# Reordering the state-space mixer of a decoder trunk into a four-part pipeline with a pinned order

## The chip, the cores and the metric

One core of one Trainium2 chip runs the whole program in one launch. The metric is the device time of a run in microseconds; a kernel's time is the median of its runs.

## The reference

A two-layer trunk over 576 tokens (512 of a prompt and 8 samples of 8 tokens), model width 1024. Order: half-step SwiGLU FFN, mixer, half-step FFN in each layer, a norm ahead of each. The mixer of layer 0 is the state-space mixer (SSD), the one that the change touches:

```python
z, xbc, dt_raw = split(h @ w_in)
xbc = silu(causal_dwconv(xbc))
xs, Bm, Cm = split(xbc)
dt = softplus(dt_raw + dt_bias); A = -exp(a_log)
y_diag = (C B^T * exp(a_i - a_j), tril) @ (x * dt)
y_off  = exp(a_i) * C @ h_start
h_next = h * exp(a_end) + B^T (x * dt * decay_end)
y = (y_diag + y_off + d_skip * x) * silu(z)
y = group_rmsnorm(y) @ w_out
```

There are 32 heads of width 64 in 8 groups (`bt` is B, `ctl` is C of a group), state size 128, chunks of 128 tokens.

## The kernel before, in words

Activations lie transposed, 128 features on the partitions by 576 tokens, and every projection tile is one `acc` accumulation in PSUM: 8 blocks of 128 features, each weight and activation split in a high and a low half and multiplied in three passes, for two halves of 288 tokens, so 48 matmuls of 128x288 (`passes`, L339). There are two `acc` tiles. Small results use `misc`, four PSUM tiles of one bank.

The SSD works by pairs of heads, 16 pairs, two per group g (j = 0, 1). Per pair there is a projection of x with a causal convolution (`conv_in`: ext L636 to L639, tails L641 and L642, bias L645, three taps L647) and one of z (`zproj`, L969). Per group there are one of B and one of C, as columns 16+g and 24+g, with `group()` (L917 to L940: transposes of B, L925, C times B, L936) and the output projection of earlier groups (`outproj`), four tiles in each pair of groups 2, 4 and 6. A group's norm takes the sum of squares `sqacc` (L949, summed by matmuls with ones, L184), an inverse root on VectorE (L189 to L197, the result is `rr`) and transposes that spread it over the partitions (`rbcast`, L218).

`pair()` (L779) is one function. It transposes the old state `nat` (L789) and copies it to `h0t` (L790), multiplies it by C (L795), loads the decay exponents `m`, masks them on GpSimd (L808 to L810), takes their exponential on ScalarE (L813) and multiplies by `cbs` (L814, L815); it transposes x (L824, L777), scales it (L827 to L835), forms the chunk states (L851) and chains them to `ht` (L857), then multiplies `ht` by C (L864), `m` by x (L871, L873), adds up `yt` (L875 to L883, with the z projection inside) and updates `nat` for the samples (L840, L843). Before the first pair, a softplus chain on VectorE (L708 to L723, then L732 to L745, from the projection of dt) gives the tile `rhs`, which `spread()` (L746, first matmul L749) multiplies out and transposes for all pairs.

A scheduler orders the instructions of each engine, each engine then runs its list in order. Only instructions marked by `keep_in_program_order` (`pin`) stay in program order among themselves; in the SSD of the kernel before these are two of the three L864 and all of L871 and L873. The small matmuls of a pair therefore lie in many short runs between the projections.

Of the kernel before, what the change touches and what calls it, by code (L numbers as in the profile page):

```python
# [49 lines left out]
def trunk(ctx, tc, x_prompt, x_sample, state_ssm, state_conv, state_pool,  # L50
# [127 lines left out]
    def rnat(accs, width):  # L178
        pt = misc()
        for c, (t0, n) in enumerate(BLOCKS):  # L180
            for h in range(0, P, 64):
                for i, acc in enumerate(accs):
                    t = t0 + h % n
                    PE.matmul(out=pt[h:h + 64, c:c + 1], lhsT=acc[:, t:t + 64], rhs=ones[:, 0:1], start=i == 0, stop=i == len(accs) - 1)  # L184
        return rstd(pt[:, 0:5], width)
# [28 lines left out]
    def rbcast(r):  # L214
        pt, pt2 = misc(), misc()
        for c, (t0, n) in enumerate(BLOCKS):
            o = pt[:, t0:t0 + n] if c < 4 else pt2[:, 0:n]
            PE.transpose(out=o, in_=r[0:n, c:c + 1].broadcast_to([n, P]), identity=ident[0:n, 0:n])  # L218
        return pt, pt2[:, 0:T - SEQ]
# [114 lines left out]
    def passes(pd, w, acts, first, last):  # L334
        for h in range(2):
            n = 0
            for (wh, wl), (ah, al) in zip(w, acts):
                for lt, a in ((wh, ah), (wh, al), (wl, ah)):
                    PE.matmul(out=pd[:, h, 0:HALF], lhsT=lt, rhs=a[:, h * HALF:(h + 1) * HALF],  # L339
                              start=first and n == 0, stop=last and n == 3 * len(acts) - 1)  # L340
                    n += 1

    def mm(pt, w, acts):
        kn = len(acts)
        for k in range(0, kn, 4):
            passes(pt, w[k:k + 4], acts[k:k + 4], k == 0, k + 4 >= kn)
# [240 lines left out]
    def ssd(tail):  # L587
# [5 lines left out]
        with ExitStack() as st:  # L593
# [31 lines left out]

            def proj(c0, w=None):
                pt = acc_tile()
                mm(pt, w or unit(win[:, :, c0:c0 + P], G), hs)
                return pt

            def conv_in(ct):
# [4 lines left out]
                V.tensor_copy(out=es[:, :, 0:3], in_=cst[:, ct].rearrange("p (b e) -> p b e", e=3))  # L636
# [5 lines left out]
                V.tensor_copy(out=tails[:, ct, 3:27].rearrange("p (b e) -> p b e", e=3), in_=es[:, :, XST - 3:XST])  # L642
                a = wk.tile([P, XW], F32, name="cacc")
                n = XS0 + NB * XST - 3
                S.activation(out=a[:, 0:n], in_=ext[:, 0:n], func=AF.Identity, scale=cw[:, ct:ct + 1], bias=col("cb", ct))  # L645
                for k in range(1, 4):
                    V.scalar_tensor_tensor(out=a[:, 0:n], in0=ext[:, k:k + n], scalar=cw[:, k * 32 + ct:k * 32 + ct + 1], in1=a[:, 0:n],  # L647
                                           op0=ALU.mult, op1=ALU.add)
                return a
# [95 lines left out]
            V.tensor_scalar(out=mh[0:32], in0=mh[0:32], scalar1=hv[0:32, 2:3], scalar2=None, op0=ALU.mult)  # L745
            def spread():  # L746
# [24 lines left out]
            pin = tc.keep_in_program_order  # L771

            def stack(pt, src):
                s3 = wk.tile([P, 2, 3, 32], F32, name="s3", bufs=1)
                S.copy(out=s3, in_=src[:, SEQ:T].rearrange("p (q s) -> p q s", q=2).unsqueeze(2).broadcast_to([P, 2, 3, 32]))
                for q in range(2):
                    PE.transpose(out=pt[0:96, q * P:(q + 1) * P], in_=s3[:, q].rearrange("p a s -> p (a s)"), identity=ident)  # L777

            def pair(g, j, bt, ctl, bnat, bblk, cbs, xst, yt):  # L779
                h0 = 4 * g + 2 * j  # L780
                pr = 2 * g + j
                nat = wk.tile([P, NB, P], F32, name="nat")
                sv = state_ssm[0, :, h0:h0 + 2].rearrange("b h p n -> (h p) b n")
                nc.sync.dma_start(out=nat, in_=sv)
                h0t = wk.tile([P, NB, P], F32, name="h0t", bufs=1)
                for q in range(2):
                    pt = misc()
                    for i in range(4):
                        PE.transpose(out=pt[:, i * P:(i + 1) * P], in_=nat[:, 4 * q + i], identity=ident)  # L789
                    (V.tensor_copy if q else S.copy)(out=h0t[:, 4 * q:4 * q + 4], in_=pt.rearrange("p (b n) -> p b n", n=P))  # L790
                pq = misc()
                for b in range(NB):
                    r = b % 4 * 32
                    o = SEQ + b // 4 * 32
                    PE.matmul(out=pq[r:r + 32, (2 + b // 4) * P:(3 + b // 4) * P], lhsT=ctl[:, o:o + 32], rhs=h0t[:, b], start=True, stop=True)  # L795
                ch = wk.tile([P, 2, P], F32, name="ch", bufs=1)
                V.tensor_copy(out=ch, in_=pq[:, 2 * P:4 * P].rearrange("p (q n) -> p q n", q=2))

                m = wk.tile([P, 2, T], F32, name="m")
                nc.sync.dma_start(out=m, in_=ad[h0:h0 + 2].unsqueeze(0).broadcast_to([P, 2, T]))  # L800
                eb = wk.tile([P, T - P], F32, name="eb", bufs=1)
                for h2 in range(2):
                    nc.sync.dma_start(out=eb[64 * h2:64 * h2 + 64], in_=ed[h0 + h2:h0 + h2 + 1, P:T].broadcast_to([64, T - P]))

# [6 lines left out]
                for h2 in range(2):  # L811
                    for c, (t0, n) in enumerate(BLOCKS):
                        S.activation(out=m[0:n, h2, t0:t0 + n], in_=m[0:n, h2, t0:t0 + n], func=AF.Exp, bias=anat[0:n, c, 0, h0 + h2:h0 + h2 + 1])  # L813
                V.tensor_tensor(out=m[:, :, 0:SEQ], in0=m[:, :, 0:SEQ], in1=cbs[:, 0:SEQ].unsqueeze(1).broadcast_to([P, 2, SEQ]), op=ALU.mult)  # L814
                V.tensor_tensor(out=ms, in0=ms, in1=cbs[0:64, SEQ:T].unsqueeze(1).broadcast_to([64, 2, 64]), op=ALU.mult)  # L815

                xdt = wk.tile([P, 4, 2, 64], F32, name="xdt", bufs=1)
                xds = xd4[pr % 2]
                xw = wk.tile([P, 4, 2, 64], F32, name="xw", bufs=1)
                pt = misc()  # L820
                pt2 = misc()
                for c, (t0, n) in enumerate(BLOCKS):
                    o = pt[0:n, c * P:(c + 1) * P] if c < 4 else pt2[0:n, 0:P]
                    PE.transpose(out=o, in_=xst[:, t0:t0 + n], identity=ident)  # L824
                stack(pt2[:, P:512], xst)
                for o, i in ((xdt, 1), (xw, 2)):
                    V.tensor_tensor(out=o, in0=pt.rearrange("s (c h p) -> s c h p", c=4, h=2),  # L827
                                    in1=bc(anat[:, 0:4, i, h0:h0 + 2], 64), op=ALU.mult)
                V.tensor_tensor(out=xds[0:64], in0=pt2[0:64, 0:P].rearrange("s (h p) -> s h p", h=2),
                                in1=bc(anat[0:64, 4, 1, h0:h0 + 2], 64), op=ALU.mult)  # L830
                xs3 = wk.tile([96, 2, 2, 64], F32, name="xs3", bufs=1)
                V.tensor_tensor(out=xs3, in0=pt2[0:96, P:3 * P].rearrange("s (q h p) -> s q h p", q=2, h=2), in1=bc(wsn[:, :, h0:h0 + 2], 64), op=ALU.mult)
                xw3 = wk.tile([96, 2, 2, 64], F32R, name="xw3", bufs=1)
                S.copy(out=xw3, in_=xs3)
                V.tensor_tensor(out=xw3[64:96], in0=xs3[64:96], in1=xw3[64:96].bitcast(F32), op=ALU.subtract)  # L835

                def update():
                    for q in range(2):
                        pt = misc()
                        PE.matmul(out=pt, lhsT=xw3[:, q].rearrange("s h p -> s (h p)"), rhs=bblk[:, q].rearrange("s b n -> s (b n)"), start=True, stop=True)  # L840
                        for i in range(4):
                            b = 4 * q + i
                            V.scalar_tensor_tensor(out=nat[:, b], in0=nat[:, b], scalar=decp[:, pr, b:b + 1], in1=pt[:, i * P:(i + 1) * P], op0=ALU.mult, op1=ALU.add)  # L843
                    nc.sync.dma_start(out=ssm_s[0, :, h0:h0 + 2].rearrange("b h p n -> (h p) b n"), in_=nat)

                if pr == 15:
                    update()

                stp = misc()
                for c in range(4):  # L850
                    PE.matmul(out=stp[:, c * P:(c + 1) * P], lhsT=bnat[:, c], rhs=xw[:, c].rearrange("s h p -> s (h p)"), start=True, stop=True)  # L851
                ht = wk.tile([P, 4, P], F32, name="ht", bufs=1)
                V.tensor_copy(out=ht[:, 0], in_=stp[:, 0:P])
                for c in range(1, 4):
                    for h2 in range(2):
                        s_ = slice(64 * h2, 64 * h2 + 64)
# [363 lines left out]
```

## Time and profile before

| | |
|---|---|
| median of 3 runs | 2354.91 us (2354.45 to 2358.41) |
| the profiled execution | 2357.4 us, span 2355.6 us, granted clock 0.987 |
| TensorE (PE) busy | 2282.7 us, 97% of the span |
| VectorE (DVE) | 1874.8 us, 80% |
| ScalarE (ACT) | 1053.1 us, 45% |
| GpSimd (POOL) | 1030.7 us, 44% |
| chain that ended last | PE 60%, DVE 9%, ACT 1%, DMA 1% |

Times in the trace count from the start of the span. The SSD runs from about 420 to 985 us. The names in a row are tiles: `misc<-ctl,ht` is a matmul into a `misc` tile from `ctl` and `ht`. A matmul's own duration overlaps its neighbours', so the distance of their starts is what a matmul takes.

### The profile page before, as it was taken

What the parts mean: (1) busy time and instruction counts of PE and PEld (TensorE: products, weight loads), DVE (VectorE), ACT (ScalarE), POOL (GpSimd) and SP (SyncE); (2) the same over time, 40 slices, a digit from 0 to 9 for tenths busy, and PEclk for the clock granted to TensorE, in tenths of its full rate; (3) what the DMA queues carried; (4) which work ended last, traced back from release to release, by engine and by line L of the source; (5) the groups of instructions that cost most, each with busy time, mean ns of one, the idle gap of its engine ahead of it and who ended that gap; (6) DMA issues with size and microseconds to landing.
All of it is one profiled execution on the core that took longest, in us unless ns stands there. A gap on an engine that the chain in (4) does not pass through costs nothing.

```text
span 2355.6 us, 43789 instructions
## 1 busy us (share of the span) xinstructions
PE 2282.7 (97%) x17572; PEld 2241.3 (95%) x17572; DVE 1874.8 (80%) x2950; ACT 1053.1 (45%) x1947; POOL 1030.7 (44%) x796
## 2 busy tenths in 40 slices
PE   8999999999999999989999999999999999999998
PEld 7999999988999999979999999999999899999997
DVE  8987778688887786798877799778876859778876
ACT  6444434455554545354444354334444344344433
POOL 4555440344444444155554535555531325555530
PEclk9999999999999999999999999999999999999999
DMA  5223222243443334412232232323222242322221
GB/s 150 90 90 108 81 90 66 62 138 110 134 135 107 118 110 113 116 57 88 90 108 82 89 99 72 108 64 99 90 81 67 67 117 83 108 68 94 90 73 59
DMA packets 272904, 222.23 MB, mean 94 GB/s; under 512 B 8322, under 2 KB 269042, under 8 KB 272701
## 3 DMA queue, kind: packets, MB, share of 16 engines
q1 hardware_dynamic: 269172, 218.04, 30.4%
q8 instruction: 139, 2.28, 0.4%
q10 hardware_dynamic: 3528, 1.39, 0.2%
q14 instruction: 65, 0.52, 0.1%
HBM read 206.46 MB, written 12.94 MB: 93 GB/s over the span
## 4 chain that ended last, share of the span: by engine, by line
PE 60%; DVE 9%; ACT 1%; DMA 1%; issue 1%; DVEq 0%; SPq 0%; ACTq 0%
PE acc L375 29%; PE acc L339 27%; DVE wh L256 1%; PE acc L554 1%; DVE cacc L647 1%; PE acc L479 1%; DVE ws L1102 1%; DVE m L814 0%; DMA rd<-in_pool_w_out 0%; PE misc L871 0%; DVE wb L318 0%; PE misc L851 0%; PE misc L864 0%; DVE glo L256 0%; ACT m L813 0%
## 5 line engine op out<-in xcount | busy, mean ns | idle before, releaser
L375 PE MATMUL acc<-wh,wb 128*128 128x288 f32 x6888 | 920.4, 295 | 4.2 <-DVE fo L380 2.3
L375 PEld LDWEIGHTS acc<-wh,wb 128*128 128x128 f32 x6888 | 916.1, 189 | 5.9 <-ACT wb L317 3.2
L339 PE MATMUL acc<-ghi,wb 128*128 128x288 f32 x2752 | 550.7, 295 | 0.3 <-DVE x L416 0.3
L339 PEld LDWEIGHTS acc<-ghi,wb 128*128 128x128 f32 x2752 | 441.2, 188 | 0.6 <-DVE x L416 0.5
L317 ACT CAST wb<-raw 128x512 fp32r<-128x512 f32 (+1 forms) x440 | 265.7, 607 | 358.8 <-PE acc L339 151.9
L339 PE MATMUL acc<-glo,wb 128*128 128x288 f32 x1376 | 404.2, 295 | 0.0
L339 PE MATMUL acc<-hhi,wb 128*128 128x288 f32 x1824 | 382.8, 300 | 2.3 <-DVE x L414 0.8
L318 POOL TENSOR_TENSOR wb<-raw,wb 128x512 fp32r<-128x512 f32 (+1 forms) x154 | 211.3, 1374 | 339.5 <-ACT wb L317 330.5
L318 DVE TENSOR_TENSOR wb<-ws,wb 128x512 fp32r<-128x512 f32 x328 | 325.8, 1004 | 15.0 <-ACT wb L317 14.9
L318 DVE TENSOR_TENSOR wb<-raw,wb 128x512 fp32r<-128x512 f32 (+1 forms) x286 | 269.3, 956 | 63.8 <-ACT wb L317 63.3
L317 ACT CAST wb<-ws 128x512 fp32r<-128x512 f32 x328 | 202.5, 621 | 241.0 <-PE acc L375 216.8
L339 PEld LDWEIGHTS acc<-hhi,wb 128*128 128x128 f32 x1824 | 297.8, 190 | 5.7 <-issue 1.6
L416 DVE SCALAR_TENSOR_TENSOR x<-acc,x 128x576 f32<-128x576 f32 x160 | 120.6, 754 | 194.8 <-PE acc L339 194.6
L339 PE MATMUL acc<-hlo,wb 128*128 128x288 f32 x912 | 273.4, 300 | 0.0
L356 POOL TENSOR_TENSOR ws<-raw,ws 128x512 f32<-128x512 f32 x82 | 151.9, 1852 | 246.0 <-DVE wb L318 241.0
L339 PEld LDWEIGHTS acc<-glo,wb 128*128 128x128 f32 x1376 | 257.9, 188 | 0.0
L318 POOL TENSOR_TENSOR wb<-rd,wb 128x512 fp32r<-128x512 f32 x128 | 174.8, 1374 | 184.0 <-ACT wb L317 183.8
L317 ACT CAST wb<-rd 128x512 fp32r<-128x512 f32 x196 | 114.0, 592 | 250.1 <-PE acc L339 219.3
L355 POOL TENSOR_TENSOR ws<-raw 128x512 f32<-128x512 f32 x82 | 124.6, 1520 | 160.4 <-DVE wb L318 160.4
L339 PEld LDWEIGHTS acc<-hlo,wb 128*128 128x128 f32 x912 | 173.0, 190 | 0.8 <-issue 0.2
L353 POOL TENSOR_TENSOR ws<-raw 128x512 f32<-128x512 f32 x82 | 128.4, 1566 | 87.5 <-DMA raw<-in_ffn_w_gate 78.4
L354 POOL TENSOR_TENSOR ws<-ws,raw 128x512 f32<-128x512 f32 x82 | 130.3, 1589 | 7.7 <-DVE wb L318 1.5
(329 smaller groups left out, 2897.5 us busy)
## 6 DMA issues: line engine op xcount, KB each, us to landing
raw<-in_ffn_w_gate SPq DMA_DIRECT2D x41, 1024.0 KB
raw<-in_ffn_w_up SPq DMA_DIRECT2D x41, 1024.0 KB
rd<-in_ffn_w_down SPq DMA_DIRECT2D x80, 512.0 KB
raw<-in_ssd_w_in SPq DMA_DIRECT2D x48, 512.0 KB
m<-ad SPq DMA_DIRECT2D x16, 576.0 KB
nat<-in_state_ssm SPq DMA_DIRECT2D x16, 512.0 KB
out<-nat SPq DMA_DIRECT2D x16, 512.0 KB
raw<-in_ssd_w_out SPq DMA_DIRECT2D x24, 256.0 KB
```

The lines of the kernel that those rows point to most:

```text
L256: V.scalar_tensor_tensor(out=o, in0=xs, scalar=g, in1=sub, op0=ALU.mult, op1=ALU.subtract)
L317: S.copy(out=hi, in_=src)
L318: (eng or V).tensor_tensor(out=lo, in0=src, in1=hi.bitcast(F32), op=ALU.subtract)
L339: PE.matmul(out=pd[:, h, 0:HALF], lhsT=lt, rhs=a[:, h * HALF:(h + 1) * HALF], start=first and n == 0, stop=last and n == 3 * len(acts) - 1)
L353: G.tensor_tensor(out=s[0], in0=blk[2], in1=blk[3], op=ALU.add)
L354: G.tensor_tensor(out=s[1], in0=s[0], in1=blk[0], op=ALU.subtract)
L355: G.tensor_tensor(out=s[2], in0=blk[2], in1=blk[0], op=ALU.subtract)
L356: G.tensor_tensor(out=s[3], in0=blk[1], in1=s[1], op=ALU.subtract)
L375: PE.matmul(out=pt[:, m, 0:HALF], lhsT=wb[:, j, k], rhs=hh[k, h][:, slot], start=n == 0, stop=n == 11)
L416: V.scalar_tensor_tensor(out=halves(x[:, d]), in0=pt[:, :, 0:HALF], scalar=scale, in1=halves(x[:, d]), op0=ALU.mult, op1=ALU.add)
L479: PE.matmul(out=pd[:, m, 0:HALF], lhsT=w[:, a, 2 * k + m], rhs=b[:, h * HALF:(h + 1) * HALF], start=n == 0, stop=n == 5)
L554: PE.matmul(out=pt[:, m, 0:HALF], lhsT=wb[:, a, k], rhs=hh[k, b][:, slot], start=q == 0 and k == a == b == 0, stop=q == 1 and k == 3 and a ...
```

## The change

The work of the SSD is the same; its order, its tiles and the engines of a few copies change. TensorE's list is the same for its first 3212 matmuls and its last 9913, of 16926.

- `pair()` becomes a generator of four parts: loads; transposes of `nat` and x into one `acc` and two `misc` tiles; C times the old state, chunk states and the matmuls of the sample update; and, after z is projected, the products with `ht` and `m`. Each of these matmuls is pinned, and one projection stands between two parts.
- The first matmul of every SSD projection is pinned (`held`), as are the first tap, the first update of `nat`, the norm's matmuls (L184, L220), and `spread()`'s first, which now comes right after the first `group()`.
- The masks and exponentials of pair p+1 (`decays`) are issued in part 2 of pair p, the exponentials pinned on ScalarE.
- L814 and L815 become one multiplication of 128x1152 (16 in place of 32). The copies ext<-cst and tails<-ext (32 each) and bnat (8) move from VectorE to ScalarE; VectorE's list goes from 2950 to 2871 instructions, ScalarE's table loads from 34 to 38.

```diff
@@ passes @@
+                    if held and first and h == n == 0:
+                        tc.keep_in_program_order(t)
@@ conv_in, taps @@
-                V.tensor_copy(out=es[:, :, 0:3], in_=cst[:, ct].rearrange("p (b e) -> p b e", e=3))
+                S.copy(out=es[:, :, 0:3], in_=cst[:, ct].rearrange("p (b e) -> p b e", e=3))
...
+            def taps(ct):
...
+                    if k == 1 and ct not in (16, 24):
+                        pin(t)
@@ spread @@
-                PE.matmul(out=pt[:, 0:P], lhsT=self_, rhs=rhs.rearrange("h a b -> h (a b)"), start=True, stop=True)
+                pin(PE.matmul(out=pt[:, 0:P], lhsT=self_, rhs=rhs.rearrange("h a b -> h (a b)"), start=True, stop=True))
@@ pair @@
+                yield
+                ph, pt, pt2 = acc_tile(), misc(), misc()
+                for b in range(NB):
+                    pin(PE.transpose(out=ph[:, b // 4, b % 4 * P:(b % 4 + 1) * P], in_=nat[:, b], identity=ident))
...
+                yield
+                pq, stp, pus = misc(), misc(), [misc(), misc()]
...
+                if later:
+                    decays(pr + 1, later)
...
+                V.tensor_tensor(out=m, in0=m, in1=cbs.unsqueeze(1).broadcast_to([P, 2, T]), op=ALU.mult)
...
+                zs = yield
...
@@ the loop over groups @@
+            conv_in(0)
+            bc_ = [bt_ctl(0, 0), bt_ctl(0, 1)]
+            taps(0)
...
+            for g in range(8):
...
+                for j in range(2):
+                    p = 2 * g + j
+                    if g < 7:
+                        conv_in((25 if j else 17) + g)
...
+                    if j == 0:
...
+                        bnat, bblk = group(bt, ctl)
...
+                    if p == 0:
+                        spread()
+                        decays(0, m_)
...
+                    next(work)
+                    next(work)
...
+                    if p < 15:
+                        conv_in(p + 1)
...
+                    if g and j == 0:
+                        r = rnat([sqacc], 256, True)
+                    next(work)
...
+                    if g % 2 == 0 and g:
+                        outproj(max(2 * g - 6, 0), 4 if g > 2 else 2, range(4 * j, 4 * j + 4))
+                    if p < 15:
+                        zs = zproj(p)
...
+                    work.send(zs)
...
+                    if g and j == 0:
+                        gnorm(g - 1, ys, r)
```

**The first place** is TensorE at `spread()`. In the list of before, the first group's products of C and B (L936, L939) are followed by three more projections ahead of `spread()`'s first matmul:

```order
L936 MATMUL misc<-ctl,bt 128x128 x4
L939 MATMUL misc<-ctl,bt 64x64
...
L339 MATMUL acc_5297<-hhi,wb 128x288
...
L339 MATMUL acc_5376<-hhi,wb 128x288
...
L339 MATMUL acc_5446<-hhi,wb 128x288
...
L749 MATMUL misc<-rhs,sel 128x128
```

In the changed list (L940 and L941 are those products, L765 is `spread()`'s first matmul):

```order
L937 MATMUL acc_5135<-ident,bt 128x128 x4
L795 MATMUL misc<-ident,s_5141 96x128 x2
L940 MATMUL acc_5135<-ctl,bt 128x128 x4
L941 MATMUL misc<-ctl,bt 64x64
L765 MATMUL misc<-rhs,sel 128x128
L772 MATMUL misc<-ident,nat 128x128
```

The last two projections ahead of `spread()` and the 32 matmuls of a third, 128 matmuls, now come after it.

**The second place** is VectorE in pair 2 (g = 1, j = 0), at the end of the norm of group 0 (L197 and L199 are the last steps of its inverse root, L970 the scaling by it, L893 and L894 the sums into `yt`). In the changed list:

```order
L976 TENSOR_TENSOR zs<-acc_6099,rb 128x576
L197 TENSOR_SCALAR rq<-rt 128x5
L899 TENSOR_TENSOR eb<-eb,misc 128x32 x2
L198 TENSOR_TENSOR rt<-rt,rq 128x5
L893 SCALAR_TENSOR_TENSOR yt<-xst,dskp,misc 128x512
L199 SCALAR_TENSOR_TENSOR rr<-rt,rr 128x5
L894 SCALAR_TENSOR_TENSOR yt<-xst,dskp,misc 128x64
```

In the list of before that last step stood 23 rows ahead of the same pair's `yt`. It now stands behind L893, which needs the matmuls L889, and on TensorE the transposes L220 of its result come right behind those:

```order
L889 MATMUL misc<-m,xdt 64x128 x8
L891 MATMUL misc<-m,xd_4653 64x64 x2
L220 MATMUL misc<-ident,rr 128x128 x4
L220 MATMUL misc<-ident,rr 128x64
L343 MATMUL acc_6203<-hhi,wb 128x288
```

It is so in pairs 2, 6 and 10; in pairs 4, 8, 12 and 14 L199 stands ahead of L893.

**The third place** is TensorE at the old state of a pair. In the list of before, in pair 2, the transposes of `nat` (L789) and the products with `h0t` (L795) with what lies between:

```order
L789 MATMUL misc<-ident,nat 128x128 x8
...
L339 MATMUL acc_6175<-hhi,wb 128x288
...
L795 MATMUL misc<-h0t,ctl 32x128 x8
L824 MATMUL misc<-ident,xst 128x128 x4
L824 MATMUL misc<-ident,xst 64x128
L777 MATMUL misc<-ident,s_5978 96x128 x2
```

In the changed list the transposes of state and x stand together, then one whole projection, and then all products of part 2:

```order
L826 MATMUL acc_5904<-ident,nat 128x128 x8
L829 MATMUL misc<-ident,xst 128x128 x4
L829 MATMUL misc<-ident,xst 64x128
L795 MATMUL misc<-ident,x_5710 96x128 x2
L343 MATMUL acc_5942<-hhi,wb 128x288
...
L184 MATMUL misc<-ones,sqacc 64x1 x10
L853 MATMUL misc<-h0t_5924,ctl 32x128 x4
L853 MATMUL misc<-h0t_5925,ctl 32x128 x4
L855 MATMUL misc<-xw,bnat 128x128 x4
L857 MATMUL misc<-bblk,xw_5927 128x512 x2
```

Between the copies' sources and the products lay 21 projection matmuls before, 48 now.

## Rows read from the trace of the kernel before

**Rows 1.** Busy time by stretch: stretch, length, each engine's busy time (PE, PEld, DVE, ACT, POOL; instructions), PE clock, DMA.

```profile
420.00:500.00 80.00, 74.11 (x568) 70.45 (x568) 55.66 (x124) 36.37 (x84) 32.03 (x34) 0.94 0.32 90
500.00:985.00 485.00, 467.93 (x3910) 444.83 (x3909) 392.13 (x877) 247.67 (x526) 201.43 (x189) 0.99 0.42 120
```

**Rows 2.** PE's waits from 420 to 1000 us: total us, times, longest.

```profile
PE misc L795 <- DVE h0t L790: 5.1, 3, 2.5
PE misc L749 <- DVE rhs L744: 4.9, 1, 4.9
PE acc L339 <- DVE ext L639: 3.8, 2, 2.3
PE misc L184 <- DVE sqacc L949: 3.0, 1, 3.0
```

**Rows 3.** Busy time by stretch, those with a PE clock below 0.9.

```profile
480.00:490.00 10.00, 10.00 (x65) 8.92 (x66) 7.70 (x15) 5.39 (x16) 5.51 (x8) 0.63 0.45 134
540.00:550.00 10.00, 8.86 (x63) 8.62 (x64) 9.63 (x32) 4.74 (x10) 2.42 (x3) 0.83 0.05 13
710.00:720.00 10.00, 7.04 (x49) 6.55 (x48) 9.78 (x22) 4.49 (x10) 5.37 (x6) 0.66 0.25 64
940.00:950.00 10.00, 9.16 (x65) 8.91 (x66) 9.21 (x28) 4.37 (x9) 2.56 (x2) 0.83 0.10 28
```

**Rows 4.** PE in order of time, before spread(): start, duration, line, idle before and its releaser.

```profile
441.68 0.40 PE L339 MATMUL acc<-hhi,wb 128*128 128x288 f32 x1
...
469.79 0.29 PE L339 MATMUL acc<-hlo,wb 128*128 128x288 f32 x1
...
472.57 0.29 PE L339 MATMUL acc<-hlo,wb 128*128 128x288 f32 x1
477.77 0.79 PE L749 MATMUL misc<-rhs,sel 64*128 64x128 f32 x2 [4.91 <-DVE rhs L744]
```

**Rows 5.** DVE in order of time, the softplus chain and what stands between.

```profile
448.82 0.23 DVE L708 TENSOR_SCALAR nat<-nat 128x160 f32<-128x160 f32 x1
448.97 0.83 DVE L647 SCALAR_TENSOR_TENSOR cacc<-ext,cw,cacc 128x600 f32<-128x600 f32 x1
...
452.20 0.31 DVE L710 TENSOR_TENSOR nat<-nat 128x160 f32<-128x160 f32 x1
...
452.99 0.18 DVE L642 COPY tails<-ext 128x24 f32<-128x24 f32 x1
453.08 2.22 DVE L711 TENSOR_TENSOR nat<-nat 128x160 f32<-128x160 f32 x1
...
472.03 0.49 DVE L723 TENSOR_TENSOR_SCAN nat<-nat 128x160 f32<-128x160 f32 x1
...
477.75 1.27 DVE L642 COPY tails<-ext 128x24 f32<-128x24 f32 x1
```

**Rows 6.** DVE groups by line from 500 to 985 us: count, busy us, mean ns, idle before.

```profile
L647 DVE SCALAR_TENSOR_TENSOR cacc<-ext,cw,cacc 128x600 f32<-128x600 f32 x79 | 81.7, 1034 | 15.4 <-POOL wb L318 7.5 <-ACT cacc L645 6.9
L843 DVE SCALAR_TENSOR_TENSOR nat<-nat,decp,misc 128x128 f32<-128x128 f32 x128 | 35.7, 339 | 0.0
L814 DVE TENSOR_TENSOR m<-m,cbs 128x1024 f32<-128x1024 f32 x14 | 22.9, 1656 | 0.3
L857 DVE SCALAR_TENSOR_TENSOR ht<-ht,decb,misc 128x64 f32<-128x64 f32 x96 | 20.7, 274 | 0.3
L875 DVE SCALAR_TENSOR_TENSOR yt<-xst,dskp,misc 128x512 f32<-128x512 f32 x16 | 11.9, 746 | 31.1 <-PE misc L871 31.1
L637 DVE TENSOR_TENSOR ext<-acc,rb 128x288 f32<-128x288 f32 x26 | 11.7, 450 | 4.7 <-PE acc L339 4.7
L642 DVE COPY tails<-ext 128x24 f32<-128x24 f32 x26 | 10.3, 398 | 0.2
L636 DVE COPY ext<-cst 128x24 f32<-128x24 f32 x25 | 8.0, 322 | 0.2
```

**Rows 7.** ACT in order of time after the chain: the table load and the exponential on which `rhs` waits.

```profile
475.28 1.28 ACT L735 ACT_TABLE_LOAD   x1 [5.82 <-DMA ad<-nat]
```

More of the change, by code (lines that the diff above doesn't have):

```diff
@@ L183, in rnat @@
                     t = t0 + h % n
-                    PE.matmul(out=pt[h:h + 64, c:c + 1], lhsT=acc[:, t:t + 64], rhs=ones[:, 0:1], start=i == 0, stop=i == len(accs) - 1)
+                    k = PE.matmul(out=pt[h:h + 64, c:c + 1], lhsT=acc[:, t:t + 64], rhs=ones[:, 0:1], start=i == 0, stop=i == len(accs) - 1)
+                    if held:
+                        tc.keep_in_program_order(k)
         return rstd(pt[:, 0:5], width)
@@ L776, in stack @@
+            def stack(pt, s3):
                 for q in range(2):
[L777 to L797, printed above, removed]
@@ L799, in pair, with decay @@
+                    pin(PE.transpose(out=pt[0:96, q * P:(q + 1) * P], in_=s3[:, q].rearrange("p a s -> p (a s)"), identity=ident))
+            def decay(p):
                 m = wk.tile([P, 2, T], F32, name="m")
[L800 to L803, printed above, removed]
+                nc.sync.dma_start(out=m, in_=ad[2 * p:2 * p + 2].unsqueeze(0).broadcast_to([P, 2, T]))
+                return m
@@ L818, in pair @@
[L818 to L821, printed above, removed]
+                        pin(S.activation(out=m[0:n, h2, t0:t0 + n], in_=m[0:n, h2, t0:t0 + n], func=AF.Exp, bias=anat[0:n, c, 0, 2 * p + h2:2 * p + h2 + 1]))
+            def pair(g, j, bt, ctl, bnat, bblk, xst, yt, m, later):
+                h0 = 4 * g + 2 * j
+                pr = 2 * g + j
+                nat = wk.tile([P, NB, P], F32, name="nat")
+                sv = state_ssm[0, :, h0:h0 + 2].rearrange("b h p n -> (h p) b n")
+                nc.sync.dma_start(out=nat, in_=sv)
+                eb = wk.tile([P, T - P], F32, name="eb", bufs=1)
+                for h2 in range(2):
+                    nc.sync.dma_start(out=eb[64 * h2:64 * h2 + 64], in_=ed[h0 + h2:h0 + h2 + 1, P:T].broadcast_to([64, T - P]))
+                yield
+                ph, pt, pt2 = acc_tile(), misc(), misc()
+                for b in range(NB):
+                    pin(PE.transpose(out=ph[:, b // 4, b % 4 * P:(b % 4 + 1) * P], in_=nat[:, b], identity=ident))
@@ new lines, in pair @@
+                stack(pt2[:, P:512], xst[1])
+                xdt = wk.tile([P, 4, 2, 64], F32, name="xdt", bufs=1)
+                xw = wk.tile([P, 4, 2, 64], F32, name="xw", bufs=1)
+                h0t = [wk.tile([P, 4, P], F32, name=f"h0t{k}", bufs=1) for k in range(2)]
+                xs3 = wk.tile([96, 2, 2, 64], F32, name="xs3", bufs=1)
+                xw3 = wk.tile([96, 2, 2, 64], F32R, name="xw3", bufs=1)
+                xds = xd4[pr % 2]
+                S.copy(out=h0t[0], in_=ph[:, 0].rearrange("p (b n) -> p b n", n=P))
@@ L835, in pair @@
                 V.tensor_tensor(out=xw3[64:96], in0=xs3[64:96], in1=xw3[64:96].bitcast(F32), op=ALU.subtract)
[L837 to L844, printed above, removed]
@@ L846, in pair @@
-                if pr == 15:
-                    update()
-                stp = misc()
-                for c in range(4):
-                    PE.matmul(out=stp[:, c * P:(c + 1) * P], lhsT=bnat[:, c], rhs=xw[:, c].rearrange("s h p -> s (h p)"), start=True, stop=True)
+                yield
+                pq, stp, pus = misc(), misc(), [misc(), misc()]
+                for b in range(NB):
+                    r = b % 4 * 32
+                    o = SEQ + b // 4 * 32
+                    pin(PE.matmul(out=pq[r:r + 32, (2 + b // 4) * P:(3 + b // 4) * P], lhsT=ctl[:, o:o + 32], rhs=h0t[b // 4][:, b % 4], start=True, stop=True))
@@ new lines, in pair @@
+                for c in range(4):
+                    pin(PE.matmul(out=stp[:, c * P:(c + 1) * P], lhsT=bnat[:, c], rhs=xw[:, c].rearrange("s h p -> s (h p)"), start=True, stop=True))
+                for q in range(2):
+                    pin(PE.matmul(out=pus[q], lhsT=xw3[:, q].rearrange("s h p -> s (h p)"), rhs=bblk[:, q].rearrange("s b n -> s (b n)"), start=True, stop=True))
+                ch = wk.tile([P, 2, P], F32, name="ch", bufs=1)
+                V.tensor_copy(out=ch, in_=pq[:, 2 * P:4 * P].rearrange("p (q n) -> p q n", q=2))
@@ new lines, in group @@
+                stack(pt2, triple(bt, "s3"))
+                for c in range(4):
+                    pin(PE.matmul(out=pa[:, 1, c * P:(c + 1) * P], lhsT=bt[:, c * P:(c + 1) * P], rhs=ctl[:, c * P:(c + 1) * P], start=True, stop=True))
+                pin(PE.matmul(out=pt2[0:64, 2 * P:2 * P + 64], lhsT=bt[:, SEQ:T], rhs=ctl[:, SEQ:T], start=True, stop=True))
+                S.copy(out=bnat, in_=pa[:, 0].rearrange("s (c n) -> s c n", n=P))
+                V.tensor_copy(out=cbs[:, 0:SEQ], in_=pa[:, 1])
@@ L935, in group @@
-                for c in range(4):
-                    PE.matmul(out=pt[:, c * P:(c + 1) * P], lhsT=bt[:, c * P:(c + 1) * P], rhs=ctl[:, c * P:(c + 1) * P], start=True, stop=True)
-                V.tensor_copy(out=cbs[:, 0:SEQ], in_=pt)
-                pt = misc()
-                PE.matmul(out=pt[0:64, 0:64], lhsT=bt[:, SEQ:T], rhs=ctl[:, SEQ:T], start=True, stop=True)
-                S.copy(out=cbs[0:64, SEQ:T], in_=pt[0:64, 0:64])
-                return bnat, bblk, cbs
+                return bnat, bblk
```

202 lines of the change are left out of this document (103 added, 99 removed).

## Prediction, on record before the changed kernel ran

> **What bounds the kernel now.** I read the stretches first. TensorE is busy 467.9 of the 485 us from 500 to 985 us, VectorE 392.1, ScalarE 247.7, GpSimd 201.4 [rows 1]. TensorE is the bound, and since the number of matmuls stays the same, the change can only win what TensorE loses there. That is 485 - 467.9 = 17.1 us of idle time, and time at the lower clock: three stretches of 10 us were granted 0.83, 0.66 and 0.83 of full speed [rows 3], so 1.7 + 3.4 + 1.7 = 6.8 us. Together 23.9 us is the most that a perfect order of the pairs could give back, 1% of the run. Outside the SSD TensorE's list is unchanged, and I put it at nothing.
>
> Next the waits: TensorE waits in few places, each for VectorE. L795 waits 5.1 us for `h0t`, up to 2.5 at once, the projections 3.8 for `ext`, L184 3.0 for `sqacc` [rows 2]. The reader is to see that these are lists out of step: `h0t` is one 0.7 us copy that stood behind other work on VectorE. The longest wait, 4.9 us at `spread()`, is of another kind: PE has done all work that lies ahead of it and the chain of the softplus is not finished [rows 2, 4]. After it the clock is 0.63 for 10 us [rows 3].
>
> **What the change removes.** The new order puts a whole projection between the transposes of a state and the products with it, 48 matmuls where 21 stood. A projection matmul takes (472.57 - 469.79) / 21 = 0.132 us [rows 4], 48 take 6.4 us. The copy has to come in that time, and the 2.5 us waits of L795 should be gone; L184 too stands a projection later. I take the whole 23.9 us as removed, **-24**, and count what remains as new waits. The other end is -8, a third of it, if most of the idle time comes from the engines' load and not from the order.
>
> **What it costs nothing or little.** The moved copies: ext<-cst and tails<-ext took 18.3 us of VectorE in 51 instructions [rows 6], about 9 if each took the shortest seen, 0.18 us [rows 5]. On ScalarE the same copies have cover: it is busy 51% of the stretch [rows 1]. Four more table loads of 1.28 us [rows 7] are 5.1 us of ScalarE, hidden by the same half. bnat and the merged multiplication save VectorE some 0.7 us a pair. None of this is on TensorE's path unless VectorE ends a wait there, so its own term is 0. If the cover were gone, the 5.1 us would be the price.
>
> **The cost at `spread()`.** It moves ahead of 128 projection matmuls, 128 x 0.132 = 17 us of work that covered the chain. From 441.68 us [rows 4] to the new place the list has 36 + 48 projection matmuls and the group's small ones: 441.7 + 11.1 + 1.8 (estimate for the small ones, from 13 at about 0.13) = 454.6 us. VectorE's chain ran from 448.82 to 472.03 us, 23.2 us without a pause, then 5.7 us through the scan, the table load and `rhs` to L749 [rows 4, 5, 7]. The new list has less between: no bnat (0.6), no z (0.7), one set of ext (0.8), a tap (0.8) and six tiny copies (0.5) fewer, 3.4 us. Ends: with every stretch by GpSimd as before (L711 took 2.22 us where L710 of the same shape took 0.31 [rows 5], some 7 us in all) `rhs` comes at 448.8 + 19.8 + 5.7 = 474.3; with none of them at 467.3. I take the middle, 470.8, since a third of the projections whose weights GpSimd splits there no longer fall into the chain. PE then waits 470.8 - 454.6 = 16 us against 5.5 (4.9 and what lies around it): **+10.5**, ends +7 and +14. The time at half clock behind it stays as it was.
>
> **New waits in the pairs.** Pinned matmuls cannot be passed, so each part now waits for its latest operand. In part 2 to 3 VectorE has, from the end of the projection of the next x, one ext set (1.0 us), eight updates of `nat` (8 x 0.28), six of `ht` (6 x 0.22), two taps (2 x 1.03) and the multiplication by `cbs` (1.64): 8.2 us, by busy time per count [rows 6]. TensorE's cover is the z projection, 6.4 us, and the small products of part 2, about 2 us: 8.4 us. In pairs with four tiles of output projection of 24 matmuls there are 12.8 us more and nothing waits. In pairs 2, 6 and 10 there is none, and there the last step of the inverse root (L199) stands behind L893, whose matmuls come just ahead of the transposes that need it: L893 takes 0.74 us [rows 6] and TensorE idles through it, the step and the way back, 1.3 us, to 2.4 with a late `ht`. I take 2.3, so 7. The four short output projections of group 2 (12 matmuls, 1.6 us each) wait for x to be added behind `nat`, `ht` and the taps on VectorE: 3. Pair 14, which has no projection ahead of part 1, 1.3; the two state transposes for the convolution 1.4; pair 0 1; lower clock after such waits 1.5. Sum **+15**. Ends: 8, if `ht` is never late, and 28, if every pair loses 1.7 us.
>
> **A rule weighed.** An operation on VectorE is stretched by GpSimd seven-fold in one row and not in the next: 2.22 us and 0.31 [rows 5]; the taps average 1.03 us where 0.83 is seen alone [rows 5, 6]. The Trainium skill ("SBUF — State Buffer", section "Who interferes with whom") has it that a VectorE instruction with two SBUF inputs and a GpSimd instruction that reads SBUF lock each other out, and that the scalar engine never waits for either. The trace agrees with the stretch. By that rule the masks of the next pair, now in part 2, would catch the merged multiplication, which has two such inputs. With 1.9 us (2.22 - 0.31) in pairs 2, 6, 10 and 14 the sum would be 7.6 us higher; I leave it out, since the mask is due long before that multiplication.
>
> **The sum.** -24 + 10.5 + 15 = +1.5 us on the profiled execution's 2357.4 us. That execution stands 2.5 us above the median of 2354.91, so against the median I predict 2356.5 us: the stalls are moved, not removed. About 0.2%, 4.7 us, can be told from no change here.
>
> **Rivals.**
> 1. *The pipeline runs clean.* VectorE's 8.2 us fit under 8.4, the copies off VectorE and the merged product take away stretches, and only the waits for the inverse root are left (3 x 1.3, and 2 for the short projections: 6), with 7 us at `spread()`: -24 + 7 + 6 = -11, or 2344 us. For it: VectorE idles 31.1 us for L871 [rows 6], so it has slack on the whole. Against: 392 of 485 us is an average, and the margin is 0.2 us.
> 2. *VectorE ends each pair* (slower). The price is in part 3 of every pair without a long output projection: `ht` comes late behind the updates of `nat`, and L881 with all matmuls pinned behind it waits. It decides when the queue of 8.2 us exceeds 8.4; by mean durations [rows 6] it is 1.0 + 8 x 0.34 + 6 x 0.27 + 2 x 1.03 + 1.66 = 9.1, and with `ch` and the steps of the root (about 1, estimate) 10.1, so 1.7 us a pair, 28 in all: -24 + 10.5 + 28 = +14.5, or 2369.5 us.
> 3. *`spread()` is the whole story* (slower). All stretches stay and `ext` or the group's small products come late, +14 there, while a third of the old idle time stays because it is not tied to order (-16): with 10 of new waits +8, or 2363 us.
> 4. *The order of the lists doesn't matter*: PE's losses come from the total of VectorE and GpSimd, and each loss comes back elsewhere (0, with `spread()` paid from the gain). This gives the forecast's number.
>
> **How the numbers follow.** Forecast, with rival 4: 0.35. Rival 1: 0.34. Rivals 2 and 3: 0.19 and 0.12. The rivals' times stand outside 4.7 us on their sides, so faster 0.34, same 0.35, slower 0.31. The range runs from -17 (-24 + 7, no new waits) to +17 (rival 2 with the gain a tenth smaller): 2338 to 2372 us. The likeliest case's own range is 2352 to 2361.
>
> **What would show it.** Right: L765 is released by VectorE after 16 us of idle, with a clock near 0.6 in the 10 us behind it; L220 waits over 1 us in pairs 2, 6 and 10; L853 does not wait for `h0t`; from 500 us to the end of the SSD TensorE's idle time is 12 to 18 us. Wrong: an idle time at `spread()` below 10 us or above 20; waits of L881 or of a projection's first matmul for VectorE in most pairs (rival 2); less than 8 us of idle time in all pairs (rival 1). If the stretch after the SSD changes its length by over 2 us, its unchanged list was no reason to put it at nothing.

## The result, and the profile after

The changed kernel ran 2372.41 us, median of 4 runs (2365.72 to 2374.38), beside 2356.34 us of the kernel before (4 runs); the ratio on record is 1.0053, 95% interval 1.004 to 1.0067, or 12.5 us. The two medians as they stand are 16 us apart (1.0068) and the two traces 17.0, so the changed kernel's place is sure to some 4 us only. On the median that the forecast was made from, 2354.91 us, that is 2367.4 us: inside the range of 2338 to 2372, though the runs' own median lies 0.4 us above it, and on the slower side, to which I gave 0.31. The likeliest case, no change, did not come about: 0.53% is beyond 0.2% with the whole interval.

The page of the changed kernel, its first part:

```profile
span 2372.6 us, 43758 instructions
PE 2286.4 (96%) x17572; PEld 2248.5 (95%) x17572; DVE 1834.5 (77%) x2871; ACT 1068.1 (45%) x2007; POOL 1024.1 (43%) x796
```

VectorE does 40 us less; TensorE's busy time is 3.7 us more. The span is 17.0 us longer. To find where, I cut both traces at one matmul behind the SSD that has the same place in both lists (it starts at 978.33 us before and at 995.95 after), and at the start of the pairs. Before, then after:

```profile
430.00:483.00 53.00, 47.11 (x353) 44.66 (x352) 38.18 (x82) 20.97 (x44) 19.76 (x25) 0.94 0.31 87
483.00:978.33 495.33, 478.26 (x3976) 454.64 (x3976) 401.50 (x893) 257.80 (x555) 210.27 (x196) 0.98 0.41 118
```

```profile
430.00:480.00 50.00, 33.20 (x241) 30.90 (x240) 30.15 (x66) 22.69 (x51) 15.85 (x22) 0.78 0.27 76
480.00:995.95 515.95, 492.78 (x4090) 472.84 (x4090) 370.73 (x828) 269.28 (x609) 204.21 (x198) 0.98 0.41 117
```

TensorE's idle time is length less busy time: 5.9 + 17.1 = 23.0 us before, 16.8 + 23.2 = 40.0 after. So 10.9 us were lost at `spread()`, 6.1 us in the pairs, and its busy time there, which holds what the lower clock costs, is the same (525.4 and 526.0 us). Behind that matmul the traces differ by 0.6 us. TensorE's waits after, to be read against [rows 2]:

```profile
PE misc L765 <- DVE rhs L758: 16.8, 1, 16.8
PE misc L882 <- DVE ht L868: 11.0, 5, 2.5
PE acc L343 <- DVE x L420: 5.7, 7, 1.5
PE misc L829 <- ACT crow L913: 1.3, 1, 1.3
PE misc L857 <- DVE rm L191: 1.1, 1, 1.1
```

The waits for `h0t`, `ext` and `sqacc` [rows 2] are gone but for 0.5 us. In their place stand `ht`, in pairs 0, 2, 6, 10 and 14, and x. Three waits of L220, 0.8 us each, come on top. The wait of L857 for `rm` (L191) is one for room: L857 writes into a `misc` tile that the norm's sums (L184) hold until `rm` has read it. At `spread()`:

```profile
454.93 0.33 PE L941 MATMUL misc<-ctl,bt 128*64 128x64 f32 x2
472.06 0.79 PE L765 MATMUL misc<-rhs,sel 64*128 64x128 f32 x2 [16.80 <-DVE rhs L758]
```

VectorE in pair 2, and what TensorE does meanwhile:

```profile
551.87 1.36 DVE L870 TENSOR_TENSOR m<-m,cbs 128x1152 f32<-128x1152 f32 x1 [0.80 <-issue]
553.14 1.86 DVE L660 SCALAR_TENSOR_TENSOR cacc<-ext,cw,cacc 128x600 f32<-128x600 f32 x1
554.93 0.27 DVE L868 SCALAR_TENSOR_TENSOR ht<-ht,decb,misc 128x64 f32<-128x64 f32 x1
555.12 1.03 DVE L195 TENSOR_TENSOR rt<-rt,rm 128x5 f32<-128x5 f32 x1
556.07 0.27 DVE L868 SCALAR_TENSOR_TENSOR ht<-ht,decb,misc 128x64 f32<-128x64 f32 x1
```

```profile
553.27 0.83 PE L881 MATMUL misc<-ctl,ht 128*128 128x128 f32 x6
556.39 0.33 PE L882 MATMUL misc<-ident,ht 128*128 128x128 f32 x1 [2.29 <-DVE ht L868]
559.84 1.38 PE L220 MATMUL misc<-ident,rr 128*128 128x128 f32 x5 [0.80 <-DVE rr L199]
```

The last two steps of `ht`, 0.27 us each, stand behind the next pair's multiplication by `cbs` (with a wait of 0.80 us before it), a tap of 1.86 us and a step of the root that took 1.03 us (0.16 in its first round, at 547.18 us).

One statement ahead of the forecast needs mending. By the lists that came out, `pin` ties an instruction to the one traced just before it on its engine, and not to all that are traced ahead of it. Of the eight updates of `nat` the first alone is marked, and what is traced just before it is the pair's own multiplication by `cbs`, not `ht`. So the scheduler could put all eight, a tap and the next pair's multiplication ahead of the last steps of `ht`. In e1_ht below, where a step of `ht` is what stands before the first update and all eight are marked, all eight come behind the six steps in every pair.

### The profile page after: what moved, and what is told of

Same layout as the page of the kernel before. It is cut to its first block, busy times and chain, and to the rows that moved or that the text cites. A ratio compares the mean times of both kernels' runs of the same rounds, so it can differ in the third digit from the quotient of the medians.

```text
span 2372.6 us, 43758 instructions
## 1 busy us (share of the span) xinstructions
PE 2286.4 (96%) x17572; PEld 2248.5 (95%) x17572; DVE 1834.5 (77%) x2871; ACT 1068.1 (45%) x2007; POOL 1024.1 (43%) x796
## 4 chain that ended last, share of the span: by engine, by line
PE 77%; DVE 16%; ACT 2%; issue 2%; DMA 2%; ACTq 0%; POOL 0%; SPq 0%; DVEq 0%; POOLq 0%
PE acc L343 37%; PE acc L381 35%; DVE wb L322 3%; DVE cacc L660 2%; DVE wh L260 2%; PE acc L485 1%; DVE m L870 1%; PE misc L889 1%; PE acc L560 1%; DVE ws L1143 1%; DVE glo L260 1%; ACT L811 0%; DVE fo L386 0%; DVE ghi L260 0%; ACT cacc L653 0%
## 5 line engine op out<-in xcount | busy, mean ns | idle before, releaser
L322 POOL TENSOR_TENSOR wb<-raw,wb 128x512 fp32r<-128x512 f32 (+1 forms) x154 | 211.2, 1375 | 321.8 <-ACT wb L321 308.3
L322 DVE TENSOR_TENSOR wb<-ws,wb 128x512 fp32r<-128x512 f32 x328 | 323.7, 998 | 15.2 <-ACT wb L321 15.1
L322 DVE TENSOR_TENSOR wb<-raw,wb 128x512 fp32r<-128x512 f32 (+1 forms) x286 | 272.8, 969 | 65.9 <-ACT wb L321 65.4
L322 POOL TENSOR_TENSOR wb<-rd,wb 128x512 fp32r<-128x512 f32 x128 | 176.2, 1386 | 182.5 <-ACT wb L321 182.5
```

The costliest lines, as they stand in the source:

```text
L322: (eng or V).tensor_tensor(out=lo, in0=src, in1=hi.bitcast(F32), op=ALU.subtract)
```

## The experiments

Ratios are to the kernel before, run on the same chip. "Against the changed kernel" is the difference of two ratios times 2355 us; with intervals of some 0.14% on either side such a difference is sure to about 4.6 us.

**e1_ht: `ht` first on VectorE.**

```diff
+                V.tensor_tensor(out=m, in0=m, in1=cbs.unsqueeze(1).broadcast_to([P, 2, T]), op=ALU.mult)
                 ch = wk.tile([P, 2, P], F32, name="ch", bufs=1)
...
-                    if b == 0:
-                        pin(t)
+                    pin(t)
```

> The changed kernel with VectorE's list alone altered: m times cbs is traced ahead of ch, and all eight updates of nat are marked, so that they and the taps behind them stand after the six steps of ht. Theory A (the waits in the pairs come from the order on VectorE): the five waits of L882 for ht, 11.0 us, and the three of L220, 2.4 us, go, with the lower clock behind them; 8 to 14 us below the changed kernel, 2358 to 2364. Theory B (VectorE is simply full there): what was late comes late elsewhere, PE waits as long for x, for the next ext or for m; within 3 us of the changed kernel.

Ratio 1.0039 (1.0025 to 1.0053), 3 us below the changed kernel: Theory B's time. The waits of L882 are gone, as A had it, but their sum came back, and L220's, which A had go too, grew from 2.4 to 5.1 us:

```profile
PE misc L857 <- DVE rm L191: 8.9, 3, 5.8
PE acc L343 <- DVE x L420: 6.1, 5, 2.0
PE misc L220 <- DVE rr L199: 5.1, 3, 2.2
```

The 5.8 us in pair 2 are one tap, which stands ahead of `rm` on VectorE. It started at 539.0 us and took 6.8 us where the other two there took 0.84; GpSimd's list for the time was

```profile
539.06 1.28 POOL L322 TENSOR_TENSOR wb<-raw,wb 128x512 fp32r<-128x512 f32 x1
540.30 0.40 POOL L808 TENSOR_SCALAR_AFFINE_SELECT m<-m 64x128 f32<-64x128 f32 x1
540.68 2.03 POOL L947 TENSOR_TENSOR bblk<-bsp,bmask 96x512 fp32r<-96x512 f32 x2
542.67 2.47 POOL L322 TENSOR_TENSOR wb<-raw,wb 128x512 fp32r<-128x512 f32 x2
```

without a pause, and the tap ended at 545.8 us, 0.7 us after the last of them.

**e2_later and e5_later: one more projection ahead of `spread()`.** In e2_later the z projection of pair 1 is computed twice, 48 matmuls too many, which I had not meant; e5_later is the same without it.

```diff
                     if g < 7:
-                        conv_in((25 if j else 17) + g)
+                        if p != 1:
+                            conv_in((25 if j else 17) + g)
...
                     if p == 0:
+                        conv_in(1)
                         spread()
...
-                        conv_in(p + 1)
+                        conv_in(p + 1 if p else 25)
```

> The changed kernel with one projection more ahead of spread(): that of the next x moves there, and the one of the next C, which opened pair 1, takes its old place. Theory A (PE has run out of work and waits for a chain that does not need it): the 16.8 us wait shrinks by the 6.4 us of 48 matmuls, to about 10.4, and the time by 5 to 7 us. Theory B (the added conv work on VectorE, ext and taps of about 3.1 us, gets into the chain of the softplus): rhs comes 3 us later and the time falls by 3 to 4 us only; and pair 1, which now has no projection ahead of its part 1, may give the rest back.

> e2_later as it was meant: there the z projection of pair 1 was computed twice, 48 matmuls or 6.4 us too many; here it is not. Theory A (the wait at spread() is lack of cover): it is as short as in e2_later, 7.6 us for 16.8, and the time 5 to 9 us below the changed kernel (ratio to the kernel before 1.0015 to 1.003). Theory B (what is won at spread() is lost in pairs 0 and 1, whose projections now stand closer to their uses): the waits for ext and ht that e2_later showed, 4.1 and 13.3 us, stay, and the time is within 3 us of the changed kernel.

e2_later: 1.0091 (1.0076 to 1.0106), 9 us above the changed kernel, of which 6.4 are the matmuls too many. e5_later: 1.0042 (1.0026 to 1.0057), 3 us below it, Theory B:

```profile
460.15 0.58 PE L343 MATMUL acc<-hhi,wb 128*128 128x288 f32 x1 [4.06 <-DVE ext L647]
477.06 0.79 PE L765 MATMUL misc<-rhs,sel 64*128 64x128 f32 x2 [7.59 <-DVE rhs L758]
506.18 0.48 PE L882 MATMUL misc<-ident,ht 128*128 128x128 f32 x1 [4.92 <-DVE ht L868]
```

Of 9.2 us won at `spread()` 4.1 went to a wait for `ext` and 2.4 to a longer one for `ht` in pair 0.

**e3_exps and b1_exps: the exponentials ahead of the six DMA issues, in the changed kernel and in the one before.**

```diff
-            spill(ad, ac)
...
             S.activation(out=e, in_=ac, func=AF.Exp)
+            spill(ad, ac)
             spill(ed, e)
```

> The changed kernel with the six DMA issues of the decay sums (L741, L743) moved on ScalarE behind the two exponentials. Theory A (the end of the chain, scan to rhs, is ScalarE's list: 1.75 + 0.90 us of issues stand ahead of the table load): the wait at spread() is 2.6 us shorter, and so is the time, by 2 to 3 us. Theory B (m's load, which reads those sums, is needed as early): the masks and exponentials of pair 0 come 0.6 to 2 us later and PE waits for m instead; no difference.

> The kernel before with the edit of e3_exps alone. If the end of the chain is ScalarE's list in this order too, the 4.9 us wait of L749 falls to about 2.3 and the time by 2 to 3 us: ratio 0.9987 to 0.9992. If the masks of the first pair then come late, no difference.

e3_exps: 1.0031 (1.0016 to 1.0046), 5 us below the changed kernel, Theory A and a little more. The wait is 4.3 us shorter where 2.6 was expected: the table load of 1.28 us now runs at 461.19 us, ahead of the scan's end:

```profile
467.77 0.79 PE L764 MATMUL misc<-rhs,sel 64*128 64x128 f32 x2 [12.53 <-DVE rhs L757]
```

b1_exps: 0.9984 (0.9973 to 0.9994), some 4 us below the kernel before:

```profile
472.93 0.79 PE L748 MATMUL misc<-rhs,sel 64*128 64x128 f32 x2 [3.92 <-DVE rhs L743]
```

`spread()` comes 4.8 us earlier (477.77 before). Its wait did not fall to 2.3 us as expected, since the scheduler also put some 24 projection matmuls fewer ahead of it and TensorE arrives 3.8 us earlier. That `rhs` comes 4.8 us earlier shows that the end of the chain is ScalarE's list in this order too.

**e4_dve: the small copies back on VectorE.**

```diff
-                S.copy(out=es[:, :, 0:3], in_=cst[:, ct].rearrange("p (b e) -> p b e", e=3))
+                V.tensor_copy(out=es[:, :, 0:3], in_=cst[:, ct].rearrange("p (b e) -> p b e", e=3))
...
-                S.copy(out=tails[:, ct, 3:27].rearrange("p (b e) -> p b e", e=3), in_=es[:, :, XST - 3:XST])
+                V.tensor_copy(out=tails[:, ct, 3:27].rearrange("p (b e) -> p b e", e=3), in_=es[:, :, XST - 3:XST])
```

> The changed kernel with the copies ext<-cst and tails<-ext back on VectorE (64 instructions of 0.18 us, 11 us of VectorE at their shortest, 4 us a quarter of them stretched). Theory A (each engine's share costs nothing unless it ends a wait): 0 to +3 us against the changed kernel, the latter where they stand ahead of ht. Theory B (the stretches by GpSimd fall on the copies and hold the taps behind them): +5 us or more, as L882 waits longer in each of its five pairs.

1.0089 (1.0074 to 1.0104), 8.5 us above the changed kernel: Theory B's time by another way. `ht` is hardly later (11.5 us in all), but L857 waits in four pairs, where it waited in one (1.1 us, pair 8):

```profile
PE misc L857 <- DVE ext L644: 4.6, 4, 1.1
545.08 1.49 DVE L846 TENSOR_TENSOR xw<-xs,xw 32x256 fp32r<-32x256 f32 x1
550.87 0.15 DVE L191 TENSOR_SCALAR rm<-misc 128x5 f32<-128x5 f32 x1
551.16 0.47 PE L857 MATMUL misc<-bblk,xw 96*128 96x512 f32 x1 [1.14 <-DVE ext L644]
```

The copy named, L644, comes only then. Each of the four starts 0.15 us after the end of L191: it is the wait for the norm's `misc` tile again. `rm` is late since L846, ahead of it on VectorE, took 1.49 to 1.55 us for 0.42 beside a weight split of GpSimd (L322); it does so in these four pairs (2, 6, 8, 10), and in the changed kernel in pair 8. What the copies hold up directly is `cbs`: in the same four pairs a copy tails<-ext ahead of it took 2.1 to 2.7 us (0.16 at its shortest), and TensorE waits 1.6 us for `cbs` in all, 0.8 before. That this delay is what moved L846 beside the split is likely, but not tested. The two traces differ by 2.4 us only, so the rest of the 8.5 us is not shown by them: the profiled execution is the fastest of its four, the changed kernel's the slowest of its four.

In this order the move was worth some 8 us, sure to about 4.6.

**e6_rnat: the norm's sums earlier.**

```diff
+                    if g and j == 0:
+                        r = rnat([sqacc], 256, True)
                     if p < 15:
                         conv_in(p + 1)
...
-                    if g and j == 0:
-                        r = rnat([sqacc], 256, True)
```

> The changed kernel with the norm's sums (L184) ahead of the projection of the next x, the third edit of c1 alone. Theory A (the waits of pairs 2, 6 and 10 are ht's, and the steps of the root only ride along): L882 waits as long as in the changed kernel, 11.0 us, L220 and L857 lose their 3.5 us, the time falls by 2 to 4 us (ratio 1.0035 to 1.0045). Theory B (the steps of the root, one by one in the list, are what makes ht late): L882 falls by half and the time by 7 us or more (ratio 1.0025 or less).

1.0049 (1.0034 to 1.0064): no difference that can be told. The mechanism is A's, `ht` keeps 10.6 us and L220 and L857 lose theirs, but the waits for x grow from 5.7 to 9.2.

**e7_own: the early exponentials undone.**

```diff
+                if pr:
+                    decays(pr, m)
                 ph, pt, pt2 = acc_tile(), misc(), misc()
...
-                if later:
-                    decays(pr + 1, later)
```

> The changed kernel with the early exponentials undone: each pair's masks and exponentials are issued in its own part 1. VectorE's list then has no multiplication of the next pair ahead of the last steps of ht in pairs 2, 6, 10 and 14. Theory A (that multiplication, 1.36 us and up to 0.8 us of wait before it, is the 2.3 us by which ht is late): the waits of L882 fall from 11.0 to 3 us or less, and the time by 6 to 9 us unless m is late instead. Theory B (early exponentials are needed): L889 waits for m in most pairs, 0.5 to 1 us each, and the time stays or rises by up to 8 us.

1.0165 (1.0149 to 1.018), 26 us above the changed kernel, beyond both theories. TensorE's waits to 1000 us:

```profile
PE misc L859 <- POOL ext L643: 11.1, 6, 1.9
PE acc L343 <- DVE x L420: 10.5, 4, 4.4
PE misc L882 <- DVE ht L868: 5.3, 5, 1.3
PE misc L881 <- DVE ht L868: 4.0, 4, 1.1
```

In pairs 2, 6, 10 and 14, where the next pair's multiplication is out of its way, `ht` is no longer waited for, so that it was part of the delay; but pairs 1, 3, 7 and 11 now wait for `ht`, and 9.3 of the 11.0 us stay. What the trace shows of the price begins at each pair's own multiplication by `cbs`, L870. It stands in VectorE's list ahead of the copies, the taps and `rm`, and now has to wait for the exponentials, which have just been issued. In pair 2 the last of them ends at 543.46 us:

```profile
L870 DVE TENSOR_TENSOR m<-m,cbs 128x1152 f32<-128x1152 f32 x16 | 21.7, 1359 | 40.0 <-issue 37.0 <-ACT m L811 3.0
543.55 1.36 DVE L870 TENSOR_TENSOR m<-m,cbs 128x1152 f32<-128x1152 f32 x1 [1.46 <-issue]
550.58 0.15 DVE L191 TENSOR_SCALAR rm<-misc 128x5 f32<-128x5 f32 x1
550.88 0.47 PE L859 MATMUL misc<-bblk,xw 96*128 96x512 f32 x1 [1.84 <-POOL ext L643]
```

VectorE stands still 40.0 us ahead of L870 in all, 9.3 in the changed kernel. The six waits of L859 (L857 in the changed kernel) end 0.15 us after L191 each time: they are the wait for the norm's `misc` tile, not for `ext`. From the copy of `cbs` (L943) to L191 it is 11.6 us in pair 2 and 9.7 in the changed kernel; of these 1.9 us 1.5 are that wait and 0.4 the subtraction `xw` (L848 there, L846 in the changed kernel), which ran beside a weight split of GpSimd. To the end of the SSD TensorE idles 37.1 us for 23.2, and its busy time is 10.2 us longer at a clock of 0.96 for 0.98. So the early exponentials, which I had not priced at all, spare VectorE's list some 31 us of standing still. How much of the 26 us that makes, no run shows by itself.

**c1_ht_rnat_exps, c2_all: the edits of e1_ht, e6_rnat and e3_exps together; with e5_later's as well.**

> Three edits on the changed kernel: the order of e1_ht, the exponentials first of e3_exps, and the norm's sums (L184) ahead of the projection of the next x instead of behind it, so that the misc tile and the steps of the root are early. Theory A (each wait is one instruction in the wrong place of a list): no waits of L882, of L857 for rm and of L220, spread() waits 12.5 us; 12 to 18 us below the changed kernel, ratio to the kernel before 0.998 to 1.0005. Theory B (VectorE loses the time to GpSimd, whatever the order): some tap is stretched by several us as in e1_ht (8.6 us for three), and the ratio stays at 1.002 or more.

> The edits of c1 with the one of e5_later. Theory A: the waits at spread() come down to about 4 us, 8 below c1; ratio to the kernel before 0.995 to 0.998, faster than both. Theory B: pairs 0 and 1 take back what spread() gives; as c1 within 3 us.

c1: 0.9991 (0.9981 to 1.0), 14.6 us below the changed kernel, Theory A's time. e1_ht and e6_rnat each gave 3 us or less alone; what both gain beyond e3_exps is (1.0031 - 0.9991) x 2355 = 9.4 us. Its pairs:

```profile
476.00:978.15 502.15, 487.30 (x4087) 469.17 (x4086) 376.10 (x826) 270.21 (x612) 207.36 (x203) 0.99 0.42 120
```

Idle 14.9 us for 23.2, clock 0.99 for 0.98, no wait of L882 or L857. L220, which A had free too, still waits, for another `misc` tile:

```profile
PE misc L220 <- DVE eb L897: 5.7, 4, 3.2
```

c2: 0.9977 (0.9967 to 0.9986), 5.4 us below the kernel before and the lowest ratio of the study. But it is only 3.3 us below c1, not 8, which is nearer to Theory B:

```profile
PE misc L764 <- DVE rhs L757: 4.4, 1, 4.4
PE misc L828 <- ACT xst L925: 4.3, 1, 4.3
```

Of the 8.1 us won at `spread()` 4.1 went to the wait for `ext`, as in e5_later, and 4.3 to one for `xst` in pair 1. And b1_exps has the kernel before at 0.9984 with one small edit, which cannot be told from c2: that the new order, mended, wins anything beyond that edit is not shown.

**c3_gnorm, c4_split: c2 with the norm's scaling behind the next projection; and with the output projection's tiles in two and two.**

```diff
                     elif j:
                         zs = zproj(p)
+                    if g and j:
+                        gnorm(g - 1, ys, r)
...
-                    if g and j == 0:
-                        gnorm(g - 1, ys, r)
```

c4_split has, on top of that:

```diff
+                    if g % 2 == 0 and g:
+                        outproj(max(2 * g - 6, 0), 4 if g > 2 else 2, range(4 * j, 4 * j + 2))
...
-                        outproj(max(2 * g - 6, 0), 4 if g > 2 else 2, range(4 * j, 4 * j + 4))
+                        outproj(max(2 * g - 6, 0), 4 if g > 2 else 2, range(4 * j + 2, 4 * j + 4))
```

> c2_all with the scaling of the group before (L220 and L970) behind the next projection instead of ahead of it. Theory A: the four waits of L220, 4.3 us, are covered by that projection's 6.4 us; 2 to 5 us below c2_all, ratio 0.996 to 0.997. Theory B: the scaling on VectorE, four operations of 0.27 to 0.75 us and two of 0.75, now stands ahead of the next pair's copies, and PE waits there; as c2_all within 2 us.

> c3_gnorm with two of the four tiles of output projection of a pair ahead of the projection of the next x, and two behind part 2. Theory A (the waits for x, 4.0 us in group 2, come from four short tiles in a row with two acc tiles): they fall to under 1.5 us; 2 to 4 us below c3_gnorm. Theory B (the additions to x get ahead of the taps and of ht on VectorE): other waits of the same sum; as c3_gnorm within 2 us.

c3: 1.0025 (1.0014 to 1.0035), 11 us above c2, worse than both theories. L220 no longer waits; the waits for x went from 4.0 to 10.6 us, and new ones came for `cbs`, 3.0, and `yn`, 2.2. c4: 0.999 (0.998 to 0.9999), 8 us below c3 but not below c2; the waits for x are still 9.5 us, so Theory A's mechanism is not what helped. The waits for `cbs` are gone; what else helped is open.

## Why the forecast was half right

The range held the result, with ends 17 us to either side; the likeliest case's own, 2352 to 2361 us, did not.

- **The wait at `spread()`: right.** Forecast 454.6 us for TensorE's arrival, 470.8 for its release, 16 us idle, +10.5; measured 455.3, 472.06, 16.8 and +10.9, with a clock of 0.51 in the 10 us behind. For the arrival, counting the work that lies ahead in the new list was enough. The release was the middle of a range of 7 us: the chain itself came out as forecast (16.3 us to the scan) but began 1.25 us later.
- **The old waits removed: right.** `h0t`, `ext` and `sqacc` are gone but for 0.5 us.
- **The new waits: the step that failed, as the size of its sum.** I put +15 (8 to 28) against -24. The pairs' idle time is 23.2 us, not the 12 to 18 that I gave as the sign of being right, and the time lost to the low clock, of which I took 6.8 us as gone, came back with it (equal busy time). Against -24 the new losses are thus 24 + 6.1 + 0.6 = some 31 us. The places were right: L882 in pairs 0, 2, 6, 10 and 14, L220 in three pairs, x in group 2. `ht` cost 11.0 us and L220 2.4 (0.8 each, where I gave over 1), where I took 9.3 for both; x 5.7 (4.7 in group 2) where I took 3; about 2.4 us (`rm`, `cbs`, `h0t`) were not in the list; and I gave the low clock 1.5 us where it cost about as much as before. The cause, too, was in part another one: in pairs 2, 6 and 10 most of the loss is a late `ht` (2.3 us each) and not the root, and in pair 14 it is `ht` as well. The queue ahead of `ht` did exceed its cover, by 1.6 to 2.5 us: rival 2's mechanism, but in five of the nine pairs without an output projection. Rival 2's 28 us counted all sixteen pairs, against its own condition, so that its time, 2369.5, lies near the result by luck.
- **The copies at nothing: wrong in this order.** e4_dve shows some 8 us. Work off the path was not free here, though its trace shows little of the price: longer waits for `cbs` behind stretched copies, and a subtraction that fell beside GpSimd's splits in three pairs more.
- **The early exponentials: not priced, worth some 26 us here.** e7_own. That -24 + 15 was not further off is luck in part: two gains were left out.
- **The rule on the shared port: the stretch is there, not in the place weighed.** The 7.6 us that I left out were for the merged multiplication; it took 1.34 to 1.36 us in fifteen pairs and 2.31 in one. Taps and the subtraction `xw` were stretched instead: one tap to 6.8 us in e1_ht, `xw` to 1.5 us in e4_dve. The Trainium skill ("SBUF — State Buffer", section "Who interferes with whom") names the lock; these rows agree with it.
- **That order alone decides** (rival 4 denied it) is shown by c1 and c2: the same work, 14.6 and 17.9 us less.

What stays open: whether e1_ht and e6_rnat gain together more than each alone. 9.4 us against some 4 for the two apart is not clear of the error of the five ratios, some 9 us; the traces' idle times in the pairs, 14.9 us in c1 against 26.7 in e1_ht and 24.0 in e6_rnat, speak for it. That each edit freed one late operand of parts 2 and 3 and met the next is argued from their waits, not tested one by one.

## What to carry to other kernels

When a list is made stiff, look up for every operand of a block what stands ahead of its producer on the producer's engine, the steps of other chains above all; here mending one such place showed the next, and only the edits together gave a clear gain. A tile that waits to be read holds up its next writer in the same way: the profile may then name whatever instruction came last, and the one that frees the tile has to be looked up. Before moving a consumer forward, add up the work that used to cover its chain; that sum was 0.7 us off here. A constraint named after program order may tie less than its name says: read the order that came out.

## What was not expected of the hardware

One VectorE tap of 0.84 us lasted 6.8 us while GpSimd ran six instructions without a pause, and ended 0.7 us after them (e1_ht): it lost not one turn but all of them. The subtraction `xw` takes 0.42 us alone and 1.5 beside one weight split; TensorE then waits 1.1 us in the same pair, in e4_dve four times and in the changed kernel once. No run takes GpSimd's instructions away, so that they are the cause is read from the coincidence in time.
